# Batched matmul: 48 of 64 pairs moved from straight-line code into a hardware loop

One Trainium2 chip, one core. The metric is the device time of one execution in microseconds (us).

## The reference

```python
x      = randn(8, 16, 256, 512)   # float32
weight = randn(8, 16, 512, 384)   # float32
out    = np.matmul(x, weight)     # 128 independent products, float32
```

The kernels cast to bf16 for the products. Two batches make a "pair": one x load of 1 MB, two weight loads of 768 KB, one store of 768 KB. There are 64 pairs.

## The kernel before

Everything is written out: 64 pairs one after the other, all loads and stores issued by one engine, SP, in program order. Tile pools hand out the buffers. A store follows its product by four pairs. The last pair is done as two single batches.

```python
    x_pool = ctx.enter_context(tc.tile_pool(name="x_pool", bufs=3))
    w_pool = ctx.enter_context(tc.tile_pool(name="w_pool", bufs=6))
    out_pool = ctx.enter_context(tc.tile_pool(name="out_pool", bufs=LAG + 3))
    # ... xb 2, xt 2, wb 4; PSUM: 2 for transposes, 3 for products
    for n, G in enumerate(groups):
        # ...
        if b % GX == 0:
            x_sb = load_x(b)                             # L60: SP issues x
        w_sb = [load_w(b + i) for i in range(G)]         # L67: then the weights
        if b % GX == 0:
            x_t = transpose_x(x_sb, RG)                  # L77 cast, L82 transposes, L86 PSUM -> SBUF
        for i in range(G):
            # ...
            nc.vector.tensor_copy(out=t[:], in_=w_sb[i][:])   # L110 weight cast
        # ... L125: 32 products of a pair; L132: two copies out of PSUM on ACT
        if len(waiting) > LAG or last:
            store(nc.sync)                               # L95: SP issues a store, four pairs late
```

## Time and profile before

| | before |
|---|---|
| time, median (lowest to highest) | 526.21 us (525.91 to 526.71, 4 runs) |
| span in the profile | 524.1 us |
| data queue's share of the 16 DMA engines | 99.9% |
| rate in the steady slices | 419 to 426 GB/s |
| busiest engine | PE, 65% |
| issue to landing of a transfer | 16.0 us |

"Landing" is the moment at which a transfer has arrived; a "slice" is one of the 40 equal parts into which the page cuts the span.

### The profile page before, as it was taken

To read this page: it belongs to the slowest core of one execution; us is meant where nothing else is said; L and a number is where in the kernel's file an instruction comes from. 1 tells how busy PE (TensorE), PEld (TensorE's weight loads), DVE (VectorE), ACT (ScalarE), POOL (GpSimd) and SP (SyncE) were. 2 spreads that over 40 slices of the span, in tenths; PEclk is the share of its full clock that TensorE was granted. 3 is DMA by queue.
4 is the path that set the end of the run, shared out by engine and by line. 5 is a ranking of instruction groups with operands and counts; after the bars stand their busy time and mean duration, and the time that the engine had idled before them with its cause. 6 is when DMAs were issued, how large, how long until landed. Compare 5 with 4: busy or idle time off the path is not lost.

```text
span 524.1 us, 7422 instructions
## 1 busy us (share of the span) xinstructions
PE 339.3 (65%) x3056; PEld 231.8 (44%) x3056; DVE 273.4 (52%) x320; ACT 103.8 (20%) x129; POOL 0.7 (0%) x6
## 2 busy tenths in 40 slices
PE   4666758558576665675857657567666586556664
PEld 2444435345444443443534435444344354344442
DVE  4565464564554645546456455564554645645543
ACT  0222122121121121212212112212121121121221
POOL 0000000000000000000000000000000000000000
PEclk9989797986978889979798887988788879898888
DMA  8999999999999999999999999999999999999996
GB/s 347 418 413 423 422 424 420 424 424 419 426 420 423 423 419 425 422 424 422 424 424 423 421 425 423 425 422 423 425 423 424 423 424 425 423 422 425 423 425 272
DMA packets 37041, 218.59 MB, mean 417 GB/s; under 512 B 4112, under 2 KB 4112, under 8 KB 28816
## 3 DMA queue, kind: packets, MB, share of 16 engines
q1 hardware_dynamic: 37008, 218.12, 99.9%
q8 instruction: 24, 0.39, 0.3%
q14 instruction: 9, 0.07, 0.0%
HBM read 167.77 MB, written 50.33 MB: 416 GB/s over the span
## 4 chain that ended last, share of the span: by engine, by line
DMA 97%; PE 1%; DVE 1%; issue 0%; ACT 0%; SPq 0%; ACTq 0%; DVEq 0%
DMA x_sb<-in_x_dram 94%; DMA w_sb<-in_weight_dram 3%; PE po L125 1%; DVE x_t L86 0%; DVE x_bf L77 0%; DVE w_bf L110 0%; ACT out_sb L132 0%; PE pt L82 0%; SPq L60 0%; ACTq L132 0%; DVEq L77 0%
## 5 line engine op out<-in xcount | busy, mean ns | idle before, releaser
L125 PE MATMUL po<-w_bf,x_t 128*64 128x384 bf16 (+1 forms) x2032 | 271.0, 400 | 136.3 <-DVE w_bf L110 135.9
L125 PEld LDWEIGHTS <-x_t 128*64 128x64 bf16 (+1 forms) x2032 | 171.5, 132 | 219.8 <-DVE w_bf L110 122.8
L132 ACT COPY out_sb<-po 128x768 f32<-128x768 f32 x128 | 102.5, 801 | 416.0 <-PE po L125 404.5
L77 DVE CAST x_bf<-x_sb 128x2048 bf16<-128x2048 f32 x64 | 78.5, 1227 | 182.0 <-DMA x_sb<-in_x_dram 182.0
L110 DVE CAST w_bf<-w_sb 128x1536 bf16<-128x1536 f32 x128 | 116.7, 952 | 1.9 <-DMA w_sb<-in_weight_dram 1.9
L86 DVE COPY x_t<-pt 128x1024 bf16<-128x1024 bf16 x128 | 83.6, 696 | 59.2 <-PE pt L82 59.2
L82 PE MATMUL pt<-identity,x_bf 128*128 128x128 bf16 x1024 | 70.3, 222 | 44.1 <-DVE x_bf L77 43.7
L82 PEld LDWEIGHTS <-x_bf 128*128 128x128 bf16 x1024 | 60.3, 115 | 67.7 <-DVE x_bf L77 63.5
L132 ACT ACT_TABLE_LOAD x1 | 1.3, 1283 | 0.7 <-PEq L156 0.7
masks.py:199 POOL TENSOR_SCALAR_AFFINE_SELECT identity<-identity 128x128 bf16<-128x128 bf16 x1 | 0.3, 294 | 0.1
masks.py:197 POOL MEMSET identity<- 128x128 bf16 x1 | 0.2, 205 | 0.3 <-POOLq L156 0.3
L156 POOL MEMSET const-bfloat16-1.0<- 128x1 bf16 x1 | 0.1, 102 | 0.0
L156 POOL MEMSET const-uint8-127<- 128x1 uint8 x1 | 0.1, 102 | 0.0
L156 POOL MEMSET const-float32-0.0<- 128x1 f32 x1 | 0.1, 99 | 0.2 <-issue 0.2
L156 POOL MEMSET const-float32-1.0<- 128x1 f32 x1 | 0.1, 99 | 0.0
## 6 DMA issues: line engine op xcount, KB each, us to landing
w_sb<-in_weight_dram SPq DMA_DIRECT2D x128, 768.0 KB, 16.0
x_sb<-in_x_dram SPq DMA_DIRECT2D x64, 1024.0 KB, 16.0
out_dram<-out_sb SPq DMA_DIRECT2D x63, 768.0 KB, 16.0
out_dram<-out_sb SPq DMA_DIRECT2D x2, 384.0 KB, 3.0
```

What stands on the lines that cost most here:

```text
L77: nc.vector.tensor_copy(out=x_bf[:, r0 : r0 + 4], in_=x_sb[:, r0 : r0 + 4])
L82: nc.tensor.transpose(pt[:, rr, ko, :], x_bf[:, r + rr, ko::KO], identity)
L86: nc.vector.tensor_copy(out=x_t[:, j : j + 2, :, :, r // RG], in_=pt[:])
L110: nc.vector.tensor_copy(out=t[:], in_=w_sb[i][:])
L125: nc.tensor.matmul(po[i * C : (i + 1) * C, rr, :N], x_t[:, r + rr, ko, c0 : c0 + CX, :], w_bf[i][:, ko, :], start=(ko == 0), stop=(ko == K ...
L132: nc.scalar.copy(out=out_sb[:, r : r + 2, :], in_=po[:, :, :N])
L156: nc = _bacc.Bacc("TRN2", target_bir_lowering=False, num_devices=1)
```

## The change

The middle 48 pairs run in a hardware loop of six iterations with eight pairs each. Buffers are fixed arrays, semaphore waits in the loop are against registers that are counted up per iteration (no barrier, that is no point where all engines wait for each other, between iterations), and the weights of a pair are loaded and cast ahead of its x. The intent: a much smaller program at the same speed. Cut to its core:

```diff
-    x_pool = ctx.enter_context(tc.tile_pool(name="x_pool", bufs=3))
-    w_pool = ctx.enter_context(tc.tile_pool(name="w_pool", bufs=6))
+    x_sb = [pool.tile([P, R, K], fp32, name=f"x_sb{s}") for s in range(4)]
+    w_sb = [pool.tile([P, KO, N], fp32, name=f"w_sb{s}") for s in range(8)]
+    out_sb = [pool.tile([P, R, N], fp32, name=f"out_sb{s}") for s in range(8)]
 ... (the other buffers likewise: pt 4 for 2, po 2 for 3)
+    def pair(b, s, lagged):
+        load_w(b, 2 * s)
+        load_w(b + 1, 2 * s + 1)
+        load_x(b, s)
+        for i in range(G):
+            cast_w(2 * s + i)
+        product(transpose_x(s, R), G, 0, [2 * s, 2 * s + 1], s, 0)
+        if lagged:
+            store(b - G * LAG, s - LAG)
+
+    for s in range(U):                                   # U = 8: eight pairs written out
+        pair(G * s, s, s >= LAG)
+    with tc.For_i(G * U, B - G * U, G * U, iteration_sync="reg_based") as b:
+        for s in range(U):
+            pair(b + G * s, U + s, True)
+    b = B - G * U
+    for s in range(U - 1):                               # seven pairs written out
+        pair(b + G * s, s, True)
 ... (the last pair as two single batches, as before)
```

## The prediction

> **What bounds the kernel now.** I read the page from the top: busy shares, slices, DMA queues, chain, DMA issues. Then I asked for the SP queue's own waits and for one pair of batches in order of time.
>
> ```profile
> PE 339.3 (65%) x3056; PEld 231.8 (44%) x3056; DVE 273.4 (52%) x320; ACT 103.8 (20%) x129; POOL 0.7 (0%) x6
> ...
> GB/s 347 418 413 423 422 424 420 424 424 419 426 420 423 423 419 425 422 424 422 424 424 423 421 425 423 425 422 423 425 423 424 423 424 425 423 422 425 423 425 272
> ...
> q1 hardware_dynamic: 37008, 218.12, 99.9%
> q8 instruction: 24, 0.39, 0.3%
> ...
> DMA 97%; PE 1%; DVE 1%; issue 0%; ACT 0%; SPq 0%; ACTq 0%; DVEq 0%
> ```
>
> No engine is over 65%, but the data queue fills 99.9% of the sixteen DMA engines, at 419 to 426 GB/s in nearly every slice, and 97% of the chain is transfers. The kernel is 218.1 MB through a full pipe: 218.1 MB at 424 GB/s is 514 us, and the other 10 of the 524.1 us span are the ramp at the start and the drain at the end.
>
> ```profile
> w_sb<-in_weight_dram SPq DMA_DIRECT2D x128, 768.0 KB, 16.0
> x_sb<-in_x_dram SPq DMA_DIRECT2D x64, 1024.0 KB, 16.0
> out_dram<-out_sb SPq DMA_DIRECT2D x63, 768.0 KB, 16.0
> ```
>
> Every transfer lands 16.0 us after it is issued, although a pair of batches (one x, two weights, one store, 3.4 MB) takes only 8.04 us (an x is issued at 243.63 and the next at 251.65). So about eight transfers are always queued: a pause of several us in the issuing queue or in an engine costs nothing, and only a real hole in the queue does. In the SP queue's waits nearly all is waiting for earlier transfers (weight loads 175.8 us, x loads 117.9, stores 85.9), which is the same fact.
>
> ```profile
> 243.63 0.33 SPq L60 DMA_DIRECT2D x_sb<-in_x_dram  x1
> 243.66 1.23 DVE L77 CAST x_bf<-x_sb 128x2048 bf16<-128x2048 f32 x1 [3.06 <-DMA x_sb<-in_x_dram]
> ...
> 244.94 1.08 PE L82 MATMUL pt<-identity,x_bf 128*128 128x128 bf16 x16 [1.53 <-DVE x_bf L77]
> ...
> 245.62 1.29 DVE L86 COPY x_t<-pt 128x1024 bf16<-128x1024 bf16 x2 [0.73 <-PE pt L82]
> 246.82 1.82 DVE L110 CAST w_bf<-w_sb 128x1536 bf16<-128x1536 f32 x2
> ...
> 248.70 4.44 PE L125 MATMUL po<-w_bf,x_t 128*64 128x384 bf16 x30 [0.35 <-DVE w_bf L110]
> ```
>
> This is the latency of one pair, which matters below: cast, transposes, copies out of PSUM, weight casts, products. The pair before it had its 30 products in 2.76 us instead of 4.44: the speed of PE alternates.
>
> [...] The kernel before increments in 256 of its 6112 PE instructions[...]; in the built loop all 768 PE instructions of an iteration increment.
>
> **The change, part by part.**
>
> Bytes and access patterns: the same loads and stores, 6 or 8 KB a partition. 0 us.
>
> More buffers (x 4 for 3, weights 8 for 6, out 8 for 7) and weights ahead of x: a transfer already waits 16 us in the queue and no engine is the bound. 0 us, except that after an x lands the weights are already cast.
>
> The loop's back edges (five) and register arithmetic: SP needs 4 issues of about 0.34 us a pair, some 1.4 us of 8.04; even if the register work tripled that, it stays ahead. DVE has 273.4/64 = 4.27 us of work a pair, PE (271.0 + 70.3)/64 = 5.3. All hidden. 0 us.
>
> Stores in the loop: the built program makes each store wait for the landing of the store before it[...]. When that one has landed, two weights and one x, 2.6 MB or 6.2 us, are still queued behind it, so the queue gets shorter, 4 to 7 transfers instead of 8, but does not run dry. 0 us, and visible: in the loop a store should land about 8 us after its issue and not 16.
>
> Entry of the loop: no barrier; the loop's counters are preset and SP goes straight on with eight transfers queued. 0 us.
>
> Exit of the loop: here is the cost. Ahead of the last eight pairs the built program has SP wait for every transfer of the loop, for the loop's last DVE, ACT and PE instruction, and then for a barrier of all engines; only then is the next load issued. The queue runs empty once. In us after the last x has landed:
> - cast starts +0.09 (an x landed at 243.57, cast at 243.66), ends +1.32; transposes +1.37; PSUM copies from +2.05 to +3.34.
> - products start after the first copy, about +2.75; 32 of them take 2.8 to 4.5 by the two paces above, so they end at 5.6 to 7.2.
> - last ACT copy 0.80 (801 ns in the groups): 6.4 to 8.0. [...]
> - waits and barrier: 0.7 (at the start of the program the engines wait 0.7 for each other)[...]: the next load goes out at +8.5.
> - the loop's last store, queued behind that x, keeps the DMA busy until +1.86 (landings of 768 KB are 1.86 apart). Idle until the issue: 6.6.
> - refilling the pipe: at the start of the program the first x was issued at 0.74 and landed at 5.63, 4.89 for 1 MB that takes 2.47 in the steady state; so 2.4 us are lost at a cold queue.
>
> Sum: 6.6 + 2.4 = 9.0 us. The end is bound by transfers again (four stores, then two half stores behind the last weights, as before), so nothing of it is won back.
>
> Instruction fetches: in the landing records of the trace the first and last of a transfer's sixteen marks are 0.4 us apart at first and 6.6 at the end; the last one steps by about 1.5 us just after instruction fetches at 190.8 and 364.7. A fetch thus delays one DMA engine by some 1.4 us, and the slowest engine met it about three times. [...] there are some 10 fetches instead of 24, and the slowest engine is spared one: -1.4. If they are fetched anew in each iteration, nothing. I take -0.6.
>
> Together 526.1 + 9.0 - 0.6 = 534.5; as a surprise in a loop is rather a cost, I say 534.8.
>
> **The rivals.**
>
> Loop free, exit hidden (526): would need the loads of the last eight pairs to be issued before the drain. The order of the built program speaks against it: one SP queue, the barrier ahead of the load. [...]
>
> An engine becomes the bound in the loop[...] DVE is the same in smaller: 4.27 plus five waits with register work, which would have to cost 0.75 us each.
>
> The shallower queue lets DMA engines run dry: the engines are up to 6.6 us apart and the store rule leaves 6.2 us. The fastest engines will idle, the slowest not, and that one sets the end. If wrong, a few tenths a pair: +5 to +15.
>
> [...]
>
> [...]
>
> **Range and chances.** Most of the doubt is the exit (7 to 12 us) and the fetches (0 to -3). 8 in 10: 530.5 to 540. Slower by 2% starts at 536.6, a hole of about 10.5 us or a small leak in the loop: 0.27. Faster by 2% would need 515.6, the bare bytes at 424 GB/s: 0.01. Within 2%: 0.72.
>
> **What would show it.** Right: one slice near three quarters of the span (seven of eight parts done, about 460 us) clearly under 424 GB/s and all others as before; there one wait of SP of 6 us or more, ended by ACT or PE, and a gap of about 11 us between the landing of the last loop store and of the next weight; stores that land after about 8 us in the loop; busy times of DVE and ACT per instruction unchanged. Wrong: slices of the loop below 415 GB/s (an engine or the store rule), a hole at each back edge, no hole at the exit, or PE's share of the loop near 90%.

Parts of the prediction are cut where no trace of this case shows what they rested on. Its sum came to 526.1 + 9.0 - 0.6 = 534.5, put at 534.8. Two terms of the exit, together 0.6 us, were the author's guess. The next load's +8.5 is the middle of the last ACT copy, 7.2, plus these 0.6, plus the 0.7 for waits and barrier. The condition for the "10 fetches instead of 24", and with it for the -1.4, was a guess too and is cut; -0.6 was taken.

## The result

The changed kernel takes 542.59 us (542.26 to 543.12, 4 runs) against 526.21: a ratio of 1.0311, 95% interval 1.0293 to 1.0329. It is slower by 16.4 us; 534.8 was predicted, with 540 as the upper end. (A ratio here is the mean time of one kernel's runs over that of the other's of the same rounds, so it is not quite the ratio of the medians quoted.)

The page of the changed kernel, lines of slices, queues and DMA issues (the last column is the time from issue to landing):

```profile
GB/s 351 419 413 422 257 371 423 424 423 422 423 425 422 423 423 423 423 424 423 424 423 423 424 424 424 422 424 425 423 423 425 424 423 221 235 425 423 422 424 325
...
q1 hardware_dynamic: 37008, 218.12, 97.5%
q8 instruction: 9, 0.15, 0.1%
...
w_sb<-in_weight_dram SPq DMA_DIRECT2D x128, 768.0 KB, 10.3
x_sb<-in_x_dram SPq DMA_DIRECT2D x64, 1024.0 KB, 12.2
out_dram<-out_sb SPq DMA_DIRECT2D x63, 768.0 KB, 7.9
```

Inside the loop, slices 7 to 33, the rate is what it was. There are two holes, not one: slices 5 and 6, where SP enters the loop, and slices 34 and 35, where it leaves it. The stores land 7.9 us after their issue, as predicted, so the queue in the loop is shorter, with no loss that the rate shows. The instruction packets fell from 24 to 9.

The stretches around both holes and the one between them, as busy time of each engine, granted clock, DMA share and rate, in the changed kernel:

```profile
core 0: us, PE busy (x) PEld busy (x) DVE busy (x) ACT busy (x) POOL busy (x), PEclk, DMA share, GB/s
45.00:75.00 30.00, 14.66 (x144) 9.55 (x144) 13.23 (x16) 4.79 (x6) 0.00 (x0) 0.82 0.85 324
75.00:452.00 377.00, 236.15 (x2256) 155.87 (x2256) 208.60 (x235) 74.33 (x93) 0.00 (x0) 0.83 1.02 424
452.00:480.00 28.00, 9.94 (x82) 6.42 (x82) 8.23 (x10) 2.40 (x3) 0.00 (x0) 0.65 0.62 234
```

**The entry.** Some of the SP queue's waits in the changed kernel (total us, times, longest us):

```profile
SPq L73 <- DMA out_dram<-out_sb: 258.9, 55, 6.2
...
SPq L67 <- DVEq L130: 14.8, 1, 14.8
...
SPq L130 <- ACT out_sb L116: 4.9, 1, 4.9
...
SPq L130 <- DVE x_t L94: 3.3, 1, 3.3
...
SPq L130 <- DMA x_sb<-in_x_dram: 2.4, 1, 2.4
```

L130 is the loop statement. The last three waits belong to the exit (below). At the entry SP waits once for 14.8 us, with its first weight load of the loop (L67), for DVE's sequencer to arrive at L130. In order of time:

```profile
46.56 0.34 SPq L73 DMA_DIRECT2D out_dram<-out_sb  x1
...
60.79 1.23 DVE L85 CAST x_bf<-x_sb 128x2048 bf16<-128x2048 f32 x1 [1.49 <-DMA x_sb<-in_x_dram]
...
62.75 1.29 DVE L94 COPY x_t<-pt 128x1024 bf16<-128x1024 bf16 x2 [0.73 <-PE pt L90]
63.37 1.58 SPq L67 DMA_DIRECT2D w_sb<-in_weight_dram  x2
...
68.02 0.96 DVE L98 CAST w_bf<-w_sb 128x1536 bf16<-128x1536 f32 x1 [3.98 <-DMA w_sb<-in_weight_dram]
...
71.73 0.96 DVE L98 CAST w_bf<-w_sb 128x1536 bf16<-128x1536 f32 x1 [2.75 <-DMA w_sb<-in_weight_dram]
74.77 1.23 DVE L85 CAST x_bf<-x_sb 128x2048 bf16<-128x2048 f32 x1 [2.08 <-DMA x_sb<-in_x_dram]
```

SP issued its last store ahead of the loop at 46.56 and then stood still until DVE had put out its last instruction ahead of the loop, at 63.37. The built program explains it: each engine adds the starting value to its own loop counter when it reaches the loop, and SP's first load in the loop waits for DVE's counter, because the load will overwrite a buffer that DVE reads. The trace's semaphore records agree: SP preset its eight transfer counters by 47.5, then waited from 48.51 to 63.26 for semaphores 114 and 113; 114 is one of those eight, and 113 was added to by DVE, at L130, at 63.21. DVE reaches the loop only after the last x ahead of it has landed (cast at 60.79). By then SP's queue is empty (last landing 62.58).

**The exit.** Of the same view, the other end:

```profile
453.79 1.23 DVE L85 CAST x_bf<-x_sb 128x2048 bf16<-128x2048 f32 x1 [1.47 <-DMA x_sb<-in_x_dram]
...
456.52 4.47 PE L109 MATMUL po<-w_bf,x_t 128*64 128x384 bf16 x32 [0.37 <-DVE x_t L94]
...
461.16 0.80 ACT L116 COPY out_sb<-po 128x768 f32<-128x768 f32 x1 [1.05 <-PE po L109]
462.58 0.82 SPq L67 DMA_DIRECT2D w_sb<-in_weight_dram  x2
...
468.16 0.96 DVE L98 CAST w_bf<-w_sb 128x1536 bf16<-128x1536 f32 x1 [11.10 <-DMA w_sb<-in_weight_dram]
...
474.49 1.23 DVE L85 CAST x_bf<-x_sb 128x2048 bf16<-128x2048 f32 x1 [3.40 <-DMA x_sb<-in_x_dram]
```

The last x is cast at 453.79, ACT ends at 461.96, the next load leaves at 462.58 and its data is cast at 468.16. In the list of waits above, SP waits here in turn for the last x (2.4), for DVE's last copy (3.3) and for ACT's (4.9); the barrier of all engines then takes up most of the 0.6 us from 461.96 to 462.58 (SP's records of it run from 462.05 to 462.47).

The size of each hole can be had from the landing records of the trace. In the steady state a pair (four landings) takes 8.05 us, so I take the time of the four landings that span a hole, less 8.05:

| changed kernel | landings, us | four landings | hole |
|---|---|---|---|
| entry | 62.58 → 67.89, 71.61, 74.65, 76.53 | 13.95 | 5.9 |
| exit | 455.57 → 468.07, 470.03, 474.39, 476.23 | 20.66 | 12.6 |

The sum is 18.5, and the span grew by 540.9 - 524.1 = 16.8, so 1.7 us were gained elsewhere (run 6 comes back to it).

### The profile page after: what moved, and what is told of

Same layout as the page of the kernel before. It is cut to its first block, busy times and chain, and to the rows that moved or that the text cites. A ratio compares the mean times of both kernels' runs of the same rounds, so it can differ in the third digit from the quotient of the medians.

```text
span 540.9 us, 8649 instructions
## 1 busy us (share of the span) xinstructions
PE 318.8 (59%) x3056; PEld 209.9 (39%) x3056; DVE 285.1 (53%) x320; ACT 103.6 (19%) x129; POOL 0.7 (0%) x6
## 5 line engine op out<-in xcount | busy, mean ns | idle before, releaser
L109 PE MATMUL po<-w_bf,x_t 128*64 128x384 bf16 (+1 forms) x2032 | 232.5, 394 | 17.4 <-DVE x_t L94 14.1
L90 PE MATMUL pt<-identity,x_bf 128*128 128x128 bf16 x1024 | 87.8, 253 | 200.2 <-DVE x_bf L85 200.2
L109 PEld LDWEIGHTS <-x_t 128*64 128x64 bf16 (+1 forms) x2032 | 135.0, 133 | 102.6 <-DVE x_t L94 23.1
L98 DVE CAST w_bf<-w_sb 128x1536 bf16<-128x1536 f32 x128 | 122.4, 958 | 91.2 <-DMA w_sb<-in_weight_dram 85.2
L90 PEld LDWEIGHTS <-x_bf 128*128 128x128 bf16 x1024 | 74.8, 126 | 223.6 <-DVE x_bf L85 223.3
L94 DVE COPY x_t<-pt 128x1024 bf16<-128x1024 bf16 x128 | 86.0, 698 | 61.6 <-PE pt L90 41.2
```

The source lines that it names most:

```text
L90: nc.tensor.transpose(t[:, rr, ko, :], x_bf[s % 2][:, r + rr, ko::KO], identity)
L94: nc.vector.tensor_copy(out=xt[:, j : j + 2, :, :, r // RG], in_=t[:])
L98: nc.vector.tensor_copy(out=w_bf[s % 4][:], in_=w_sb[s % 8][:])
L109: nc.tensor.matmul(p[rows, rr, :N], xt[:, r + rr, ko, (i0 + i) * C : (i0 + i + 1) * C, :], w_bf[ws[i] % 4][:, ko, :], start=(ko == 0), sto ...
```

## The experiments

My theory after the result: two holes in the transfers, one at the entry (DVE's late counter lets the queue run dry) and one at the exit (drain, computing, barrier, refill), less some gain from fewer instruction fetches. Rivals: the new order and buffers cost something; an entry or exit costs because of a branch or cold instructions, whatever stands before it; the loop's inside leaks. Every kernel gave the right result. The first four ran on one chip (before: 526.17), the last four on another (before: 526.32).

**1. No loop.** Everything else as in the changed kernel.

```diff
-    with tc.For_i(G * U, B - G * U, G * U, iteration_sync="reg_based") as b:
+    for b in range(G * U, B - G * U, G * U):
         for s in range(U):
```

> The changed kernel with the loop written out: same buffers, same order, no loop. My theory is that the 16.4 us are two holes in the transfers, one at the entry of the loop (5.9 us by the landings) and one at its exit (12.6 us), less about 1.7 us from fewer instruction fetches (9 packets of 16 KB instead of 24). Written out, all three go: 526.2 +- 0.7 us, no slice under 410 GB/s but the first and last, 24 instruction packets. Rival: the order (weights ahead of x) and the buffers carry part of the difference; then it is at least 1.5 us away from 526.2. Second rival: waits on registers or on the store before cost inside the loop; then it also falls to 526, but the slices inside the loop of the changed kernel (422 to 425 GB/s) leave no room for it.

Measured: 525.70 us (525.47 to 525.93), ratio 0.999 (0.9976 to 1.0004), 24 instruction packets of 16 KB. The order, the buffers and the weights ahead of x cost nothing measurable; all 16 us belong to the loop. The same middle stretch as above, in this kernel:

```profile
75.00:452.00 377.00, 233.31 (x2234) 151.59 (x2231) 206.59 (x233) 74.95 (x94) 0.00 (x0) 0.84 1.02 423
```

423 GB/s written out, 424 in the loop; PE takes 233.31/2234 = 104.4 ns an instruction here and 236.15/2256 = 104.7 in the loop, DVE 887 and 888 ns. By the semaphore marks in the traces, 4673 of the changed kernel's 6112 PE instructions (products, transposes and weight loads) increment a semaphore and 256 of run 1's. Register work and these increments cost the two engines nothing measurable.

**2. Loads three pairs ahead.** Same loop, same buffers; what changes is when SP has to pass into the loop and out of it, relative to the computing.

```diff
     def pair(b, s, lagged):
-        load_w(b, 2 * s)
-        load_w(b + 1, 2 * s + 1)
-        load_x(b, s)
+        load(b + G * AHEAD, s + AHEAD)      # AHEAD = 3; the same three loads, of a later pair
 ... (the first three pairs are loaded ahead of everything, the last loads fall away)
```

> Loads issued three pairs ahead of the pair that is computed, with the same buffers and the same loop. My theory of the entry: the issuing queue may pass into the loop only when DVE has reached it, because DVE adds the preset to its own counter when it gets there, after its last pair ahead of the loop; the queue of transfers has run dry by then. With three pairs already queued there is no hole at the entry (0 instead of 5.9). At the exit the computing is long done when the last load lands, so only barrier, issue and refill are left: about 1.3 + 3.6 + 1.9 = 6.8 us instead of 12.6. Together 542.6 - 5.9 - 5.8 = 531 (529.5 to 533). Rival for the entry (a fetch or a branch on the issuing queue stalls it): the hole stays, 537. Rival for the exit (the drain itself costs it, not the computing): 537 as well, and the two are told apart by the slices.

Measured: 531.18 us (530.25 to 531.72), ratio 1.0093. Its line of rates:

```profile
GB/s 352 420 417 419 420 423 422 421 423 423 422 424 422 425 423 423 424 423 425 422 424 422 424 424 425 423 424 421 422 425 423 421 424 424 423 224 396 424 422 303
```

There is no hole at the entry (0.0 us by the landings) and one of 7.1 at the exit, where 6.8 was expected. The wait at the entry has turned round: now DVE waits there for SP,

```profile
65.68 1.83 DVE L98 CAST w_bf<-w_sb 128x1536 bf16<-128x1536 f32 x2 [7.96 <-SPq L138]
```

and its 7.96 us cost nothing, because the transfers go on. So the entry is not expensive as such; it is expensive when the engine that issues transfers waits there for an engine that waits for the last transfer. At the exit the computing is out of the way (the next load leaves 0.7 us after the last landing, where 1.3 had been put in for barrier and issue); what is left, 6.4 us, is refilling: the first weight lands 4.1 late, the second 0.3, the x 2.1. This is the fastest version with a loop: within 2% of the kernel before, but still 0.9% slower than it (interval 1.0079 to 1.0107).

**3. Two loops directly behind each other** (three iterations each).

```diff
-    with tc.For_i(G * U, B - G * U, G * U, iteration_sync="reg_based") as b:
+    with tc.For_i(G * U, 4 * G * U, G * U, iteration_sync="reg_based") as b:
         ...
+    with tc.For_i(4 * G * U, B - G * U, G * U, iteration_sync="reg_based") as b:
+        ...
```

> The loop split into two of three iterations each, one directly behind the other. My theory: the second entry finds every engine just released from the barrier, so DVE adds its preset at once and the entry costs next to nothing; a second exit hole of 12.6 us comes on top: 542.6 + 12.6 = 555 (553.5 to 556.5). Rival (an entry costs 5.9 us whatever precedes it): 561.

Measured: 560.70 us (559.47 to 562.33). By the time alone the rival's 561 is right and mine is wrong. By the landings the two exits cost 13.4 and 10.0 us and the first entry 5.3, and the second entry is inside the 13.4. What fills up the rest stands at the end of the program: the last transfer landed at 552.28 and the span ended at 555.58, 3.3 us later instead of 1.0 as in the other runs, with small instruction packets at 553.1 and 555.6; and time minus span is 4.0 us here, 1.8 in the changed kernel. Together 4.5 us, in this one profile, that have nothing to do with an entry. This reading was made after the fact, so it was put to the test in run 8.

**4. Two loops with eight written-out pairs between them** (two and three iterations).

```diff
-    with tc.For_i(G * U, B - G * U, G * U, iteration_sync="reg_based") as b: ...
+    with tc.For_i(G * U, 3 * G * U, G * U, iteration_sync="reg_based") as b: ...
+    for s in range(U):
+        pair(3 * G * U + G * s, U + s, True)
+    with tc.For_i(4 * G * U, B - G * U, G * U, iteration_sync="reg_based") as b: ...
```

> The loop split into two (two and three iterations) with eight pairs written out between them, so one more exit and one more entry with work in front of it. My theory: both holes once more, 542.6 + 12.6 + 5.9 = 561 (559.5 to 563). Rival (the holes belong to the first branch, to cold instructions or to the place in the program): clearly less, 550 or under. Compared with the adjacent loops it gives the cost of an entry alone: theory 5.9.

Measured: 562.26 us (560.50 to 563.61), ratio 1.0675, as the theory has it. The holes by the landings: entry 5.6, exit 11.5, entry 6.2, exit 12.3. They repeat wherever they are put, so neither the place nor a first use makes them.

**5. The changed kernel again**, for the second chip.

> The changed kernel unaltered, as the yardstick on the chip of this call: 542.6 us (542.0 to 543.3).

Measured: 544.25 us (541.48 to 544.65), ratio 1.0329: somewhat above what I expected, and wider. Holes of 5.5 and 12.1; the span of 541.7 less these is 524.1, so in this profile nothing was gained elsewhere.

**6. A body of 24 pairs, two iterations.**

```diff
-    with tc.For_i(G * U, B - G * U, G * U, iteration_sync="reg_based") as b:
-        for s in range(U):
+    with tc.For_i(G * U, B - G * U, 3 * G * U, iteration_sync="reg_based") as b:
+        for s in range(3 * U):
```

> 24 pairs in the loop's body and two iterations instead of eight pairs and six. Two holes as in the changed kernel. My theory of the missing 1.7 us: [...] 9 packets of 16 KB are fetched instead of 24, and each one fetched delays a DMA engine by about 1.4 us. With about 2400 PE instructions in the body [...] about 24 packets again, and 1 to 2 us more than the changed kernel, 543.6 to 544.6. Rival (the gain has another source, such as the shorter queue): within 0.5 us of the changed kernel, whatever the packets; or fewer than 15 packets, and then nothing is said.

Measured: 545.43 us (544.99 to 546.71), ratio 1.0367 (1.0352 to 1.0382) against 1.0329 (1.0305 to 1.0352) of run 5: 0.0038, or 2.0 us, the intervals just touching. That is above the 543.6 to 544.6 expected, which was reckoned from 542.6 and not from run 5's 544.25. Its instruction packets:

```profile
q8 instruction: 26, 0.43, 0.3%
```

The small body was not fetched anew on its later passes: in the changed kernel no instruction packet falls between 112.1 and 464.3 us. With the large body there are 26 packets instead of 9. The counts are as expected; the reason given for them was not shown. What fewer packets are worth is less clear: span less holes is 522.4, 524.1 and 523.2 us in the three profiles with 9 packets and the loop as in the change (the changed kernel, runs 5 and 7), 527.0 here with 26, but 524.0 in run 1 with 24 and no loop. The sign fits; that sum gives 0 to 1.7 us for the change itself. In the large body SP's code grew too, which this run does not separate.

The landing records narrow it. From the 9th to the 55th x, 46 pairs:

| | us for 46 pairs | pairs with a step | a pair, the steps left out |
|---|---|---|---|
| changed kernel, 9 packets | 370.98 | none | 8.065 |
| run 5, 9 packets | 371.49 | one, 8.78 | 8.060 |
| run 7, 9 packets | 370.83 | none | 8.062 |
| run 6, 26 packets, loop | 373.45 | two, 9.28 and 9.47 | 8.061 |
| run 1, 24 packets, no loop | 372.36 | two, 9.61 and 9.57 | 8.027 |

Both steps of run 1 come just behind an instruction packet (194.6 and 366.0 us), and so do both of run 6 (154.2 and 307.1); most packets leave no step, and the one of run 5 has no packet near it. So inside the loop the change gains 0.9 to 1.5 us on run 1. It is the difference of two things: no steps, some 3 us saved, and about 0.035 us more for each pair, some 1.6 us lost in all loops, which 424 against 423 GB/s does not show. The cause of the latter is not shown.

**7. The first store behind the loop one pair later.**

```diff
     for s in range(U - 1):
-        pair(b + G * s, s, True)
+        pair(b + G * s, s, s != 0)
+        if s == 1:
+            store(b - G * LAG, -LAG)
```

> Behind the loop the first pair issues no store and the second issues two. In the changed kernel the first x behind the loop lands 4.36 us after the weights before it, where 2.45 is normal. Theory: the first transfers that run in both directions after a cold start[...] are slow; then the first x is normal here (2.4 to 2.8) and the slow one comes with the first store, one pair later; the time stays within 1 us of the changed kernel. Rival: the first x after a refill is slow whatever stands behind it; then it lands 4 us or more after its weights here too.

Measured: 542.95 us (540.92 to 543.78), ratio 1.0320, so unchanged. DVE's casts of weights and x behind the exit in this kernel:

```profile
467.20 0.96 DVE L98 CAST w_bf<-w_sb 128x1536 bf16<-128x1536 f32 x1 [0.92 <-DMA w_sb<-in_weight_dram]
...
469.69 1.23 DVE L85 CAST x_bf<-x_sb 128x2048 bf16<-128x2048 f32 x1 [1.52 <-DMA x_sb<-in_x_dram]
...
477.87 1.23 DVE L85 CAST x_bf<-x_sb 128x2048 bf16<-128x2048 f32 x1 [2.80 <-DMA x_sb<-in_x_dram]
```

The first x comes 2.49 us after its weights, as in the steady state (470.12 to 474.49, 4.37 us, in the changed kernel). The next x, the one with the first store right behind it, is the slow one: it landed 4.19 us after its weights. So behind an exit the slow transfer moves with the first store. This is no general rule: behind the entry of the changed kernel, with the first store likewise behind the first x, the second weight is the late one (3.71 us after the first, steady 1.88) and the x only 0.6 late. Why is not shown.

**8. Two adjacent loops with other code behind them** (two and three iterations, sixteen pairs written out at the end; as in run 3, with eight more pairs written out in place of the last iteration).

> Two loops directly behind each other once more (two and three iterations), with sixteen pairs written out behind them. In the first such run the last transfer landed at 552.28 but the span ended at 555.58, with instruction packets at 553.1 and 555.6: 2.2 us of the span, and 2.2 more between span and time, belong to a fetch at the end of the program and not to the loops. With other code behind the loops that fetch should fall elsewhere. Theory (an entry right behind an exit costs about 1 us or nothing): 554.5 to 557, the span ending 1.0 us after the last landing. Rival (each entry costs 5.9): 561.

Measured: 557.16 us (557.03 to 557.33), 0.16 above my range and far from 561. The last transfer landed at 554.60 and the span ended at 555.54, 0.9 later: the 3.3 us at the end of run 3 are not there. Against run 5 on the same chip one exit with an entry behind it costs 557.16 - 544.25 = 12.9 us, hardly more than an exit alone (11.1 to 12.6 in runs 5, 6 and the changed kernel). By the landings of its own profile the exit with an entry behind it is 12.5 and the exit alone 12.0. An entry right behind a barrier costs next to nothing, as the theory of the late counter says.

## Why the prediction was wrong

Step by step, in the order of its sum:

- *What bounds it, bytes, buffers, order: 0.* Right: run 1 is 525.70.
- *Back edges, register work, increments: 0.* Right for the engines, the same time per instruction on PE (104.4 and 104.7 ns) and DVE (887 and 888), and 424 GB/s through all six iterations; the 0.035 us more a pair (run 6) are the small rest that it missed.
- *Stores wait for each other, queue shorter, 0.* Right, with the 8 us of landing that it named (7.9). The rival of DMA engines running dry, a few tenths a pair, did not come.
- *"Entry of the loop: no barrier; the loop's counters are preset and SP goes straight on with eight transfers queued. 0 us."* Wrong: 5.9 us. This is the step that failed. I had looked at the counters that SP itself presets, those of the transfers, and taken the others for the same; DVE's and ACT's are preset by DVE and ACT, when they get there (at 63.21 and 66.36 us). No barrier stands in the program, but two waits across engines make one. Of the 5.9, 0.8 pass between the last landing (62.58) and the issue (63.37); the other 5.1 are the refilling of an empty queue. Run 2 shows the path: with transfers queued ahead, 0.0.
- *Exit: 9.0.* The mechanism is right, the size is not: 12.6. Its first part was well sized, the idle time until the next issue, 462.58 - 455.57 = 7.0 for 6.6. The mis-sized term is the refill, 2.4 in the sum: the first weight landed 5.49 after its issue, 3.6 more than its steady 1.86, and the x was 1.9 late on top (4.36 for 2.45). I had read the refill from the program's start, where the first transfers have no store near them; run 7 shows that, behind an exit, the x just ahead of the first store is what is late.
- *Fetches: -0.6, between nothing and -1.4.* 9 packets came where some 10 were named, none of them from 112.1 to 464.3 us. Inside the loop the net gain is 0.9 to 1.5 us on run 1; that this is so near the -1.4 is partly luck, since two steps of some 1.5 us were saved, and not one, and the slower pairs took half of it back.

Two slips in the prediction's readings change nothing: 243.63 to 251.65 is 8.02 us and not 8.04, and the place of the exit "near three quarters of the span" should read seven eighths, as its own 460 us says; slices 34 and 35 are there.

5.9 + 12.6 - 1.7 = 16.8 is the growth of the span by construction, since the 1.7 is what remained; independent of that are runs 2 and 4, whose times (531 and 561) were computed from the two holes before they ran.

The failed step was within reach: the list of waits of the first load in the loop names DVE's loop counter, and the place where that counter is preset stands in DVE's own instructions. I read where SP's counters were set and stopped.

What stays open: why a pair takes 0.035 us more in a loop, and which of the first transfers on an empty queue are slow, and why.

## What to carry to other kernels

In a kernel bound by transfers, ask of each new synchronization not how long it lasts but whether the issuing queue can stand there with nothing queued behind it; here a hole cost the idle time plus 5.1 us (entry) to 6.4 us (exit of run 2) of refilling. In the changed kernel and runs 5 and 6 that made 5.5 to 5.9 us for the entry and 11.1 to 12.6 us for the exit; with loads three pairs ahead it was 0.0 and 7.1. A loop without barriers between its iterations still has an entry and an exit: for each wait of the issuing engine look up which engine posts it and what that engine must first have done. Issuing loads some pairs ahead of the computing hid the entry altogether and took 5.5 us off the exit.
